# A two-layer RWKV-7 / short-conv / Fourier / MoE block: input projection and units in one written order on all queues, another scratch image for the 32x32 block inverses

## Chip, cores and metric

The kernel runs on one core of a Trainium2 chip. The metric is device time in microseconds (us) from the first to the last instruction of one execution; lower is better.

## The reference, cut to what matters

Two layers. In each, tokens (256 of context, 1024 of latents, 1024 channels) are normalised and multiplied by one wide matrix, the input projection (2944 columns). The first 1920 columns feed a bidirectional RWKV-7 time mixing with 8 heads of 64 channels:

```python
z = z + (shift(z) - z) * mu_shift            # neighbour tokens
r, k, v, lw_f, lw_b, la_f, la_b, lg = split(z)
kk = k * k_k / norm(k * k_k)                 # per head
decay = exp(-exp(-softplus(-(w0 + tanh(lw) @ w2)) - 0.5))
a = sigmoid(a0 + la @ a2);  k_dir = k * (1 + (a - 1) * k_a)
# per direction, over tokens t:
s = s * decay_t - (s @ kk_t) (kk_t * a_t)^T + v_t k_t^T;  y_t = s @ r_t
```

The other columns feed a gated convolution and a Fourier mixing. Then come the output projection, a router and a mixture of 32 experts (top 2), all in float32 accuracy.

## The kernel before, in words

`inproj` does the projection. `project(j, ...)` multiplies one block of 128 output channels (j = 0 to 22) with all 1280 tokens, in chunks of 256, 512 and 512 columns; each chunk is 8 x 3 matmuls, since a float32 product is made from high and low parts (`hh`, `hl`, `wh`, `wl`). `shifted` then makes the token shift of a block by DMAs through the tile `zs`.

The time recurrence is done in chunks of 64 tokens (C). What a chunk needs beforehand is computed in 16 **units** per layer: a unit is (p, hf, d), that is two heads, half of the tokens (10 chunks, 640 tokens) and one direction. The stages of a unit:

- `gates`: two small matmul pairs (`ps<-lw,w` and `ps<-la,a`), tanh on ScalarE (ACT), a scan on VectorE (DVE), two exponentials.
- `heads` (every second unit): the normalised kk. `factors`: the operand tiles `ar` and `bk`. Half of `bk` (lines 532, 533), the sum of `kd` and the spread of `inv` are made on GpSimd (POOL).
- `attn`: 20 products `ps<-ar,bk`, masked by DVE into the two tiles `X` (line 566), and 10 transposes of `bk` into `bt`. DMAs take `ar`, `X` and `bt` to DRAM scratch (`rlD`, `abD`, `btD`, `gD`).

Between them `Pace.feed` puts projection matmuls ("52 units of 512 columns a pass"); I call the time from one unit's gates to the next unit's gates a **pass**.

Each chunk also needs the inverse of a 64x64 triangular matrix, taken from `X` through `gD`. `inverse` inverts 32x32 diagonal blocks, three units at a time (at u = 3, 6, 9, 12), by 60 instructions in a row on GpSimd, one block to a partition. It reads and writes them in an image whose rows of 32 numbers are 64 numbers apart (`diag`), and a transposed copy goes to a second image (`xD`). `merge` loads a unit's blocks again, joins them by 40 small matmuls (`pq<-zt`), and writes `abD`. For units 12 and 13 the inverse runs on VectorE into the tile `lw`, for units 14 and 15 on GpSimd into the tile `v`, in `beside`, which runs next to the scan.

`scan` is the recurrence itself, 20 steps in each direction, and is fed by big loads (`st`) from the scratch. Its first matmuls (`pR<-st`, line 1061) wait for the loads and for two memsets of state on GpSimd (line 1106). After it come `outproj`, `experts` and `combine`.

What sets the order: every engine runs its instructions in program order, and SyncE (SP) issues nearly all DMAs, also in order. In `inproj` the order was made by the framework's scheduler from its own estimates; `in_order` (used in `experts`) pins the written order on all engines but SP.

Of the kernel before, what the change touches and what calls it, by code (L numbers as in the profile page):

```python
# [19 lines left out]
P = 128  # L20
# [20 lines left out]
Q_FIRST, Q_UNIT, Q_TAIL, Q_SCAN, Q_LATE, Q_AT = (40, 35), ((52, 35), (49, 24)), ((40, 60, 40), (20, 60, 40)), 10, 40, (1, 8)  # L41
# [7 lines left out]

Q = 32 * C + 32  # L50
U_ = 2 * Q

# [10 lines left out]
class Pace:  # L63
# [8 lines left out]

    HOLD = 1e9
# [17 lines left out]
    def after(self):  # L91
        return self.tc.issue_after(self.last)

    def one(self, ctx):
        cost = self.cost
        try:
            self.cost = self.stream.send(ctx)
        except StopIteration:
            self.cost = None
        for x in self.later:  # L100
            x[0] -= cost
        while self.later and not self.open and (self.cost is None or self.later[0][0] <= 0):
            self.later.pop(0)[1]()
# [20 lines left out]
class K:  # L124
# [30 lines left out]
    def in_order(self):  # L155
# [9 lines left out]
        for i in traced[start:]:  # L165
            if i.engine == mybir.EngineType.SP:
                continue
# [116 lines left out]
    def weights(self, l, j):  # L284

        hp = self.hp
        wr = hp.tile([P, KD, P], F32, name="wr")
        self.nc.sync.dma_start(wr, self.a["w_in"][l, j])
# [59 lines left out]
    def inproj(self, l, last):  # L348
# [13 lines left out]
        nc.vector.tensor_scalar(om, self.vec("mu", 0, 15), -1.0, 1.0, op0=OP.mult, op1=OP.add)  # L362
        oka = sp.tile([P, 4], F32, name="oka")
        nc.vector.tensor_scalar(oka, self.vec("ka", 0, 4), -1.0, 1.0, op0=OP.mult, op1=OP.add)
# [21 lines left out]
        def project(j, use, ctx=True):  # L386

            wh, wl = self.pre.pop(j) if j in self.pre else self.weights(l, j)
            for c0, n in NCK if ctx else NCK[1:]:
# [11 lines left out]
                pace.open = False  # L401
                between()

# [32 lines left out]
        def shifted(j, name, bufs=1, ctx=True):  # L436
# [14 lines left out]
            else:  # L451
                nc.gpsimd.memset(z[:, :LC], 0.0)
            ts = slice(0, T) if ctx else slice(LC, T)
            nc.scalar.activation(z[:, ts], z[:, ts], AF.Copy, scale=om[:, j:j + 1])
            nc.vector.scalar_tensor_tensor(z[:, ts], zs[:, ts], self.vec("mu", j), z[:, ts], op0=OP.mult, op1=OP.add)
            return z
# [20 lines left out]
        def heads(p, hf, k, inv):  # L477

            kk = un.tile([P, HT], F32, name="kk", bufs=2)
            nc.gpsimd.tensor_copy(kk.rearrange("q (t e d) -> q t e d", e=2, d=64),  # L480
                                 inv[:, 5 * hf:5 * hf + 5, :, None].to_broadcast([P, 5, 2, 64]))
            ps = bank()
            for t in range(5):
                nc.tensor.matmul(ps[:, t * P:(t + 1) * P], kk[:, t * P:(t + 1) * P], self.ident, start=True, stop=True)
# [7 lines left out]
        def gates(p, hf, d, lw, la):  # L492
# [6 lines left out]
            for i, (w, src, dst) in enumerate(((w2, lw, sg), (a2, la, aa))):  # L499
# [8 lines left out]
                nc.vector.tensor_scalar(dst, dst, 0.5, 0.5, op0=OP.mult, op1=OP.add)  # L508
            rev = slice(None, None, -1) if d else slice(None)
            nc.vector.tensor_tensor_scan(flat(sg)[:, rev], rst, flat(sg)[:, rev], 0.0, op0=OP.mult, op1=OP.add)  # L510
            E = un.tile([P, HC, C], F32, name="E")
            Ei = un.tile([P, HC, C], F32, name="Ei")
            nc.scalar.activation(E, sg, AF.Exp, scale=-CC)
            nc.scalar.activation(Ei, sg, AF.Exp, scale=CC)
            return aa, E, Ei

        def factors(p, hf, d, r, k, kk, g, kds):
            aa, E, Ei = g
            rev = slice(None, None, -1) if d else slice(None)
            e0 = 0 if d else C - 1  # L520
            nc.vector.tensor_copy(self.wc[d][:, p, hf * HC:(hf + 1) * HC], E[:, :, e0])
            kd = un.tile([P, HC, C], F32, name="kd", bufs=2)
            nc.scalar.activation(kd, aa, AF.Identity, bias=oka[:, p:p + 1], scale=self.vec("ka", p))
            nc.vector.tensor_tensor(kd, kd, cv(k, hf), op=OP.mult)
            kds.append(kd)
            nc.vector.tensor_tensor(aa, aa, Ei, op=OP.mult)


            ar = un.tile([P, 2, HC, C], F32, name="ar")
            bk = un.tile([P, HC, 2, C], F32, name="bk")  # L530
            lo, hi = slice(0, 64), slice(64, 128)
# [10 lines left out]
            nc.vector.tensor_tensor(ar[:, 1], cv(r, hf), E, op=OP.mult)  # L542
            if len(kds) == 2:
                nc.gpsimd.tensor_tensor(kds[0], kds[0], kds[1], op=OP.add)
                nc.gpsimd.tensor_tensor(kds[0], kds[0], cv(r, hf), op=OP.mult)
                nc.sync.dma_start(self.prD[p][:, hf * HT:(hf + 1) * HT], flat(kds[0]))
            return ar, bk

        def attn(p, hf, d, ar, bk):

            GR = ((0, 5), (5, 5))
            half = lambda e: slice(64 * e, 64 * e + 64)
            img = slice(hf * HC, (hf + 1) * HC)

            Xs = [un.tile([P, 2, HC, C], F32, name="X", bufs=2) for _ in range(2)]
            for c0, n in ((0, 4), (4, 3), (7, 3)):
                ps = bank().rearrange("q (e c s t) -> q e c s t", e=2, s=2, t=C)
                for c in range(n):
                    for e in range(2):
                        h = half(e)  # L560
                        mm = nc.tensor.matmul(ps[:, e, c], bk[h, c0 + c].rearrange("q s t -> q (s t)"), ar[h, :, c0 + c, :],
                                              start=True, stop=True)
                pace.point(mm, W_ATTN)
                for e in range(2):
                    mv = msk[:, d, e].rearrange("q (s t) -> q s t", s=2)
                    nc.vector.tensor_tensor(Xs[e][:, :, c0:c0 + n].rearrange("q s c t -> q c s t"), ps[:, e, :n],
                                            mv[:, None].to_broadcast([P, n, 2, C]), op=OP.mult)
            for e in range(2):
# [1392 lines left out]
```

## Time and profile before

| | us |
|---|---|
| median of 3 runs (3510.56 to 3526.83) | 3520.9 |
| the profiled execution | 3516.07 |
| its span | 3514.3 |
| first gates to first scan matmul, layer 0 / layer 1 | 463.0 / 457.0 |
| first to last gates (15 passes), layer 0 / layer 1 | 364.7 / 354.0 |
| last gates to first scan matmul (the tail), layer 0 / layer 1 | 98.3 / 103.0 |

The last three lines are differences of start times of rows below. Busy shares of the span: TensorE (PE) 89%, DVE 65%, ACT 53%, POOL 32%. TensorE's share counts matmuls with modelled ends, so it also reads high where the clock is low.

### The profile page before, as it was taken

The page shows a single profiled execution, that of the slowest core. Times are in us where ns is not written, and L with a number is a line of the kernel's source. Part 1 is how long each engine was busy: PE and PEld are TensorE (multiplying, and loading weights), DVE is VectorE, ACT ScalarE, POOL GpSimd, SP SyncE. Part 2 cuts the span into 40 slices and gives each one's busy share as a digit, 9 for nine tenths or more (in the row PEclk, how much of TensorE's full clock was granted, in tenths as well). Part 3 has the DMA queues.
Part 4 walks back from the last instruction along what each step waited for, and adds up shares of the span by engine and source line. Part 5 has one row for each costly group of instructions (what it writes and reads, how often), then busy time and mean ns, then how long its engine had stood idle before and what let it go on. Part 6 is the DMA issues. An engine that isn't in the chain of part 4 may idle for free. (4 is left out here: it accounts for less than half of the span.)

```text
span 3514.3 us, 59519 instructions
## 1 busy us (share of the span) xinstructions
PE 3131.3 (89%) x22452; PEld 2446.8 (70%) x22452; DVE 2270.9 (65%) x3540; ACT 1850.8 (53%) x2856; POOL 1141.2 (32%) x1084
## 2 busy tenths in 40 slices
PE   6998888798898999999979988877887989999997
PEld 3777667576676777788736766656666867778884
DVE  4265566233477899988852565563244779998885
ACT  4343433335333777788743434324353467778883
POOL 0026675411222222333200266673013222233330
PEclk8998888899998999999989998778899989999998
DMA  6668889879755999999966678989896488899996
GB/s 248 213 159 176 183 181 194 231 218 328 236 195 191 354 348 339 370 386 382 360 244 231 156 177 177 186 187 247 225 303 199 152 308 327 345 368 376 380 387 230
DMA packets 708063, 922.39 MB, mean 262 GB/s; under 512 B 335074, under 2 KB 561259, under 8 KB 657852
## 3 DMA queue, kind: packets, MB, share of 16 engines
q1 hardware_dynamic: 669456, 871.05, 77.6%
q0 software_dynamic: 38304, 47.49, 4.0%
q8 instruction: 179, 2.93, 0.3%
q14 instruction: 112, 0.92, 0.1%
q10 hardware_dynamic: 12, 0.00, 0.0%
HBM read 726.92 MB, written 203.23 MB: 265 GB/s over the span
## 5 line engine op out<-in xcount | busy, mean ns | idle before, releaser
L176 DVE TENSOR_TENSOR hl<-ld,hl 128x1024 fp32r<-128x1024 f32 x733 | 892.2, 1270 | 30.0 <-ACT hl L175 29.7
L175 ACT ACTIVATE hl<-ld 128x1024 fp32r<-128x1024 f32 x796 | 793.0, 1058 | 22.8 <-PE pR L1572 14.9
L1572 PE MATMUL pR<-hl,wk 128*128 128x512 f32 x1560 | 455.3, 400 | 0.0
L1572 PE MATMUL pU<-hl,wk 128*128 128x512 f32 x1560 | 446.7, 395 | 0.0
L1596 PE MATMUL pA<-hl,wk 128*128 128x512 f32 x1560 | 388.6, 404 | 12.9 <-DVE wk L176 8.9
L397 PE MATMUL pb<-hh,wh 128*128 128x512 f32 (+1 forms) x1000 | 393.0, 394 | 6.7 <-ACT r L430 3.9
L397 PE MATMUL pb<-hl,wh 128*128 128x512 f32 (+1 forms) x1000 | 389.3, 390 | 0.0
L397 PE MATMUL pb<-hh,wl 128*128 128x512 f32 (+1 forms) x1000 | 387.5, 388 | 1.3 <-DVE wl L176 1.3
L1596 PEld LDWEIGHTS pA<-hl,wk 128*128 128x128 f32 x1560 | 290.5, 191 | 98.2 <-ACT wk L175 19.2
L1572 PEld LDWEIGHTS pU<-hl,wk 128*128 128x128 f32 x1560 | 294.4, 189 | 68.0
L1572 PEld LDWEIGHTS pR<-hl,wk 128*128 128x128 f32 x1560 | 288.0, 189 | 61.3 <-ACT wk L175 0.6
L176 POOL TENSOR_TENSOR hl<-ld,hl 128x1024 fp32r<-128x1024 f32 x63 | 176.2, 2797 | 376.0 <-ACT hl L175 376.0
L1603 POOL DMA_INDIRECT yb<-wk,sca x65 | 103.2, 1588 | 472.3 <-ACT wk L1602 437.6
L397 PEld LDWEIGHTS pb<-hh,wh 128*128 128x128 f32 x1000 | 200.3, 200 | 74.2 <-issue 14.8
L397 PEld LDWEIGHTS pb<-hl,wh 128*128 128x128 f32 x1000 | 201.3, 201 | 39.0 <-issue 11.1
L397 PEld LDWEIGHTS pb<-hh,wl 128*128 128x128 f32 x1000 | 200.9, 201 | 35.6 <-issue 3.1
L1276 PE MATMUL pA<-hl,wk 128*128 128x512 f32 x864 | 222.3, 407 | 3.4 <-ACT wk L175 3.3
L1100 POOL DMA_DIRECT2D yD<-yt x72 | 58.1, 807 | 411.5 <-ACT yt L1099 381.1
L1276 PEld LDWEIGHTS pA<-hl,wk 128*128 128x128 f32 x864 | 160.4, 192 | 43.8 <-issue 6.4
L1088 DVE TENSOR_TENSOR tm<-pR,ST 128x256 f32<-128x256 f32 x76 | 32.1, 423 | 237.3 <-PE pR L1083 222.9
L175 ACT ACTIVATE wk<-pm 128x256 fp32r<-128x256 f32 (+1 forms) x195 | 89.0, 456 | 178.2 <-PE pm L1586 115.6
L607 POOL TENSOR_TENSOR gt<-gt,tmp 120x30 f32<-120x30 f32 (+14 forms) x240 | 170.1, 709 | 17.7
(422 smaller groups left out, 5368.2 us busy)
## 6 DMA issues: line engine op xcount, KB each, us to landing
ld<-in_exp_gu SPq DMA_DIRECT2D x260, 1024.0 KB
ld<-in_exp_dn SPq DMA_DIRECT2D x130, 1024.0 KB
st<-rlD SPq DMA_DIRECT2D x80, 512.0 KB
wr<-in_w_in SPq DMA_DIRECT2D x46, 512.0 KB
rlD<-ar SPq DMA_DIRECT2D x64, 320.0 KB
rlD<-X SPq DMA_DIRECT2D x64, 320.0 KB
btD<-bt SPq DMA_DIRECT2D x64, 320.0 KB
st<-abD SPq DMA_DIRECT2D x40, 512.0 KB
```

Of the source, the lines that this page charges most:

```text
L175: nc.scalar.activation(hi, src, AF.Copy)
L176: (eng or nc.vector).tensor_tensor(lo, src, hi.bitcast(F32), op=OP.subtract)
L397: mm = nc.tensor.matmul(ps[:, :n], w[:, k, :], h[:, k, c0:c0 + n], start=(k == 0 and i == 0), stop=(k == KD - 1 and i == 2))
L607: eng.tensor_tensor(gt[:, 0:j, j + 1:32], gt[:, 0:j, j + 1:32], tv, op=OP.add)
L1088: nc.vector.tensor_tensor(tm, RS[:, 1], ST[d], op=OP.add)
L1100: nc.gpsimd.dma_start(self.yD[d][:, ch * C:(ch + 1) * C, :], yt.rearrange("q p d -> q (p d)"))
L1276: nc.tensor.matmul(ps, oo[o][:, k, :], w[k][w_][:, fs], start=(k == 0 and q == 0), stop=(k == KD - 1 and q == 2))
L1572: nc.tensor.matmul(o, x.xT[xi][:, kk, :], w[wi][:, k, :], start=(kk == 0 and i == 0), stop=(kk == KD - 1 and i == 2))
L1596: nc.tensor.matmul(x.y[n], x.h[:, hi_, f, :], dw[wi][:, 0, n * 512:(n + 1) * 512], start=(f == 0 and i == 0), stop=(f == 3 and i == 2))
L1603: nc.gpsimd.indirect_dma_start(out=yb, out_offset=bass.IndirectOffsetOnAxis(ap=x.sca, axis=0), in_=o, in_offset=None, bounds_check=2 * T - ...
```

## The change

It keeps the mathematics and does the following:

1. The whole of `inproj` up to the scan stands in `in_order(True)`, which pins the written order on all queues, SP's DMA issues too. Stages became generators, and the loop places them between groups of projection matmuls by hand. Weights are fetched two blocks ahead.
2. A pass is now: gates of u+1 at its end; `factors`, `attn` of u-1, `heads`, `operands` of u; then the DMAs of `X`, the inverse, the merge.
3. The merge's loads stand in the middle of a pass, its matmuls some 16 projection matmuls later. It makes the transposed block itself (20 more small matmuls), so `xD` and its DMAs are gone.
4. The image: a 32x32 block is 4 KB in one piece, so `inverse` loads and stores whole rows of 4 KB; `attn` writes three 32x32 parts per head (`diag` twice, `corner`) in runs of 128 bytes where it wrote one 64x64 part in runs of 256 bytes.
5. All of `bk`, `kd` and `kk` is made on DVE; one affine step of the gates moves to ACT, one is folded into later operations. The inverse of units 12 and 13 moves from DVE to GpSimd.

```diff
-    def in_order(self):
+    def in_order(self, issue=False):
...
-            if i.engine == mybir.EngineType.SP:
+            if i.engine == mybir.EngineType.SP and not issue:
                 continue
...
-                nc.vector.tensor_scalar(dst, dst, 0.5, 0.5, op0=OP.mult, op1=OP.add)
+                if i == 0:
+                    nc.scalar.activation(dst, dst, AF.Copy, bias=0.5, scale=0.5)
+                yield
...
-            nc.gpsimd.tensor_tensor(bk[hi, :, 0, :], kd[hi], Ei[hi], op=OP.mult)
-            nc.gpsimd.tensor_tensor(bk[hi, :, 1, :], kk[hi, :, rev], aa[hi, :, rev], op=OP.mult)
-            nc.vector.tensor_tensor(bk[lo, :, 1, :], kd[lo], Ei[lo], op=OP.mult)
-            nc.vector.tensor_tensor(bk[lo, :, 0, :], kk[lo, :, rev], aa[lo, :, rev], op=OP.mult)
+            nc.vector.scalar_tensor_tensor(bk[:, :, 1], kk[:, :, rev], 0.5, aa[:, :, rev], op0=OP.mult, op1=OP.mult)
+            for e in range(2):
+                h = slice(64 * e, 64 * e + 64)
+                nc.vector.tensor_tensor(bk[h, :, 2 - 2 * e], kd[h], Ei[h], op=OP.mult)
...
+            for e in range(2):
+                h = slice(64 * e, 64 * e + 64)
+                nc.sync.dma_start(self.rlD[d][e][hf * HC:(hf + 1) * HC, h, p, :].rearrange("m q x -> q m x"),
+                                  ar[h].rearrange("q s (n c) t -> q (s n) (c t)", c=2))
...
+                m = 2 * place[p, hf, d] + e
+                for b in range(2):
+                    q = slice(32 * b, 32 * b + 32)
+                    nc.sync.dma_start(self.diag(m, b), X[h, 0][q, :, q])
+                nc.sync.dma_start(self.corner(m), X[h, 0][0:32, :, 32:64])
...
-                m = (2 * place[p, hf, d] + e) * HC
-                nc.sync.dma_start(self.mats(self.gD, m, HC), X[h, 0])
...
+            img = self.blocks(j0, n)
+            nc.sync.dma_start(gt, img)
...
-                nc.sync.dma_start(self.diag(self.xD, j0, n), xt)
+                nc.sync.dma_start(img, gt.rearrange("q i a -> q (i a)"))
...
-                    inverting = inverse(12, 2, nc.vector, by_l)
...
+        with self.in_order(True):
...
+                a_ = attn(*units[u - 1], *ops) if u else iter(())
+                f_ = factors(p, hf, d, k, g)
+                next(f_)
+                go(a_, 5)
+                next(f_)
+                go(a_, 5)
+                merging = merge(u - 7, lambda: un.tile([P, 1024], F32, name="zt")) if 7 <= u < 16 else None
+                go(a_, 5)
+                f = self.whole(f_)
+                if u % 2 == 0:
+                    kk, kds = heads(p, hf, k, invs[p]), []
+                    pace.free(2 * n)
+                go(a_, 5, 4)
+                ops = operands(p, hf, d, r, kk, f, kds)
+                self.whole(a_)
+                if u % 3 == 0 and u:
+                    if inverting:
+                        inverting()
+                    inverting = inverse(u - 3, 3, nc.gpsimd) if u < 15 else inverse(12, 2, nc.gpsimd, by_l)
+                if merging:
+                    m = merging(nullcontext())
+                    go(m, 6, 6)
+                    self.whole(m)
...
+                    g_ = gates(*units[u + 1], *lw)
+                    go(g_, 7, 7)
+                    g = self.whole(g_)
```

**SP, a pass in the middle of layer 0.** Names are destination and source of a DMA; `nD` is the image of corners. Before:

```order
L573 DMA rlD_61<-X 64x10x128
L575 DMA abD_64<-X 64x5x128
L578 DMA gD<-X 64x10x64
L573 DMA rlD_62<-X 64x10x128
L575 DMA abD_64<-X 64x5x128
L578 DMA gD<-X 64x10x64
L589 DMA btD_66<-bt 128x5x128 x2
L573 DMA rlD_59<-ar 64x10x128
```

Now:

```order
L617 DMA btD_65<-bt 128x5x128 x2
L574 DMA rlD_61<-ar 64x10x128
L574 DMA rlD_62<-ar 64x10x128
L580 DMA prD<-kd 128x640
L625 DMA gD<-X 32x10x32 x2
L626 DMA nD<-X 32x10x32
L627 DMA rlD_59<-X 64x10x128
L629 DMA abD_63<-X 64x5x128
L625 DMA gD<-X 32x10x32 x2
L626 DMA nD<-X 32x10x32
L627 DMA rlD_60<-X 64x10x128
L629 DMA abD_63<-X 64x5x128
```

The DMAs that read the two X tiles stood first and are six; they are ten now and stand behind those of `bt`, of `ar` and of `kd`.

**DVE, the same place, now** (`bk` and `ar` are the operands that the next unit's products read, X the masked products of the last one):

```order
L602 TENSOR_TENSOR X<-ps_5021,msk 128x4x2x64 x2
L602 TENSOR_TENSOR X<-ps_5040,msk 128x3x2x64 x2
L664 MEMSET zt 32x10x32 x2
L602 TENSOR_TENSOR X<-ps_5062,msk 128x3x2x64 x2
L548 SCALAR_TENSOR_TENSOR aa<-aa,Ei 128x640
L549 TENSOR_TENSOR kd<-kd,k 128x640
L559 SCALAR_TENSOR_TENSOR bk<-kk,aa 128x10x64
L562 TENSOR_TENSOR bk<-kd,Ei 64x10x64 x2
L565 TENSOR_TENSOR ar<-kk,E 128x10x63
L566 COPY ar<-kk 128x10
L570 TENSOR_TENSOR ar<-r,E 128x640
```

All six masks now stand ahead of all operand work, in every pass.

**POOL, the end of layer 0's units.** `v` is the inverse of units 14 and 15, `lw` that of 12 and 13 (60 instructions each, cut here), `st` the state memsets of the scan. Before:

```order
L601 MEMSET v 80x32
L605 TENSOR_TENSOR v<-v 80x30
L607 TENSOR_TENSOR v<-v 80x30
...
L605 TENSOR_TENSOR v<-v 80x238
L1106 MEMSET st_5247 64x256 x2
L1106 MEMSET st_5258 64x256 x2
```

Now:

```order
L647 TENSOR_TENSOR v<-v 80x30
L647 TENSOR_TENSOR lw<-lw 80x210
L649 TENSOR_TENSOR v<-v 80x30
L649 TENSOR_TENSOR lw<-lw 80x10x21
...
L649 TENSOR_TENSOR lw<-lw 80x30
...
L649 TENSOR_TENSOR v<-v 80x14x17
L1193 MEMSET st_5801 64x256 x2
L1193 MEMSET st_5812 64x256 x2
```

Before, 27 rows of `v` stand ahead of the memsets; now all 60 of `lw` and 34 of `v` do (in layer 1: 15 before, 60 and 30 now).

## Rows read from the trace of the kernel before

**Rows 1.** Stage: us; busy PE, PEld, DVE, ACT, POOL; PE clock; DMA; GB/s

```profile
335.00:540.00 205.00, 168.25 (x1475) 133.88 (x1474) 115.61 (x149) 78.65 (x117) 142.61 (x171) 0.86 0.88 187
```

**Rows 2.** Timeline of PE: gates of units 0, 1, 15 in both layers

```profile
175.02 1.34 PE L502 MATMUL ps<-lw,w 64*128 64x320 f32 x4
186.17 1.07 PE L502 MATMUL ps<-lw,w 64*128 64x320 f32 x3
539.69 1.34 PE L502 MATMUL ps<-lw,w 64*128 64x320 f32 x4
1961.14 1.07 PE L502 MATMUL ps<-lw,w 64*128 64x320 f32 x3
1974.57 1.34 PE L502 MATMUL ps<-lw,w 64*128 64x320 f32 x4
2315.17 1.07 PE L502 MATMUL ps<-lw,w 64*128 64x320 f32 x3
```

**Rows 3.** PE's waits, 175 to 540, then 1961 to 2315: us, times, longest

```profile
PE pq L645 <- DMA zt<-xD: 22.6, 9, 12.8
...
PE ps L561 <- POOL bk L533: 16.9, 4, 7.4
```

**Rows 4.** Timeline of SP, layers 0 and 1: start, length of issue

```profile
439.08 0.62 SPq L636 DMA_DIRECT2D zt<-xD  x1
...
1989.31 0.63 SPq L573 DMA_DIRECT2D rlD<-X  x1
1989.99 0.64 SPq L575 DMA_DIRECT2D abD<-X  x1
...
2001.79 1.79 SPq L573 DMA_DIRECT2D rlD<-ar  x2
...
2309.43 5.18 SPq L622 DMA_DIRECT2D xD<-zt  x1
...
2329.66 0.59 SPq L578 DMA_DIRECT2D gD<-X  x1
```

**Rows 5.** Timeline of DVE: a mask that waited for an X tile

```profile
2333.17 1.16 DVE L566 TENSOR_TENSOR X<-ps,msk 128x512 f32<-128x512 f32 x2 [3.33 <-DMA gD<-X]
```

**Rows 6.** DVE by form, 175 to 640: count, busy us, mean ns

```profile
L566 DVE TENSOR_TENSOR X<-ps,msk 128x384 f32<-128x384 f32 x64 | 32.5, 549 | 24.2 <-PE ps L561 24.2
L535 DVE TENSOR_TENSOR bk<-kk,aa 64x640 f32<-64x640 f32 x16 | 22.9, 1429 | 0.2
L566 DVE TENSOR_TENSOR X<-ps,msk 128x512 f32<-128x512 f32 x32 | 20.6, 682 | 12.4 <-PE ps L561 12.4
L534 DVE TENSOR_TENSOR bk<-kd,Ei 64x640 f32<-64x640 f32 x16 | 17.3, 1081 | 20.4 <-PE ps L583 20.3
L526 DVE TENSOR_TENSOR aa<-aa,Ei 128x640 f32<-128x640 f32 x16 | 15.6, 975 | 0.0
L537 DVE TENSOR_TENSOR ar<-kk,E 128x630 f32<-128x630 f32 x8 | 10.4, 1300 | 0.0
```

**Rows 7.** Timeline of DVE: masks and an operand step between two inverses on POOL

```profile
328.19 1.02 DVE L566 TENSOR_TENSOR X<-ps,msk 128x384 f32<-128x384 f32 x2
...
334.56 0.82 DVE L535 TENSOR_TENSOR bk<-kk,aa 64x640 f32<-64x640 f32 x1
```

**Rows 8.** Tails: first rows of the inverses, first scan matmuls

```profile
579.56 0.20 DVE L605 TENSOR_TENSOR lw<-lw 80x30 f32<-80x30 f32 x1 [3.96 <-DMA lw<-gD]
...
638.00 0.45 PE L1061 MATMUL pR<-st,st 128*64 128x64 f32 x2 [11.46 <-DMA st<-vE]
...
2418.16 0.44 PE L1061 MATMUL pR<-st,st 128*64 128x64 f32 x2 [12.17 <-DMA st<-vE]
```

**Rows 9.** POOL: `v` alone in its stretch (layer 1), then mean ns by line

```profile
2405.00:2443.00 38.00, 0.00 (x0) 0.00 (x0) 0.00 (x0) 0.00 (x0) 31.09 (x61) 0.68 1.02 282
...
L607 POOL TENSOR_TENSOR gt<-gt,tmp 120x30 f32<-120x30 f32 (+14 forms) x120 | 86.0, 716 | 8.9
...
L607 POOL TENSOR_TENSOR v<-v 80x30 f32<-80x30 f32 (+14 forms) x30 | 15.5, 515 | 2.4
```

More of the change, by code (lines that the diff above doesn't have):

```diff
@@ L71, in __init__ @@
         self.open = False
+        self.pinned = True
     HOLD = 1e9
@@ L101, in one @@
             x[0] -= cost
-        while self.later and not self.open and (self.cost is None or self.later[0][0] <= 0):
+        while self.later and (self.pinned or not self.open) and (self.cost is None or self.later[0][0] <= 0):
             self.later.pop(0)[1]()
@@ L567, in attn @@
                                             mv[:, None].to_broadcast([P, n, 2, C]), op=OP.mult)
+                yield
+            for c0, n in GR:
+                ps = bank().rearrange("q (e c d) -> q e c d", e=2, d=C)
+                for c in range(n):
+                    for e in range(2):
+                        h = half(e)
+                        mm = nc.tensor.matmul(ps[:, e, c], left(e, c0 + c), self.ident[h, h], start=True, stop=True)
+                pace.point(mm, W_ATTN)
+                bt = un.tile([P, 5, P], F32, name="bt", bufs=2)
+                nc.scalar.activation(bt[:, :n].rearrange("q c (e d) -> q c e d", e=2),
+                                     ps[:, :, :n].rearrange("q e c d -> q c e d"), AF.Copy)
+                ch = slice(hf * HC + c0, hf * HC + c0 + n)
+                nc.sync.dma_start(self.btD[d][ch, :, p, :].rearrange("c q x -> q c x"), bt[:, :n])
+                yield
             for e in range(2):
@@ L633, in merge, with steps @@
             for e, (r, o) in enumerate(ro):
-                m = (2 * u + e) * HC
-                nc.sync.dma_start(AM[64 * e:64 * e + 64], self.mats(self.gD, m, HC))
-                nc.sync.dma_start(XP[r], self.mats(self.xD, m, HC)[lo, :, lo])
-            def work(ctx):
+                m = 2 * u + e
+                nc.vector.memset(AM[o, :, lo], 0.0)
+                nc.sync.dma_start(AM[r, :, hi], self.corner(m))
+                for b, (rows, cols) in enumerate(((r, lo), (o, hi))):
+                    nc.sync.dma_start(AM[rows, :, cols], self.diag(m, b))
+            def steps(ctx):
+                pq = qp.tile([P, 512], F32, name=bank)[:, :HC * 32].rearrange("q (u t) -> q u t", t=32)
+                for c in range(HC):
+                    for r, o in ro:
+                        with ctx:
+                            nc.tensor.matmul(pq[r, c, :], AM[r, c, lo], self.ident[r, r], start=True, stop=True)
+                        ctx = nullcontext()
+                for r, o in ro:
+                    nc.scalar.activation(XP[r], pq[r], AF.Copy)
+                yield
                 for st in range(2):
@@ L679, in conv @@
+            yield from shifted(8 + p, "v", then)
         def conv(i):
@@ L832, in inproj @@
                 if u < 15:
-                    inverting = inverse(u - 3, 3, nc.gpsimd)
-                else:
-                    inverting = inverse(12, 2, nc.vector, by_l)
-            if 6 <= u < 15:
-                merging = merge(u - 6, zt)
-            pace.feed(Q_UNIT[last][u > 9])
-        attn(*prev)
-        mg = [merge(9 + i, new, ("pq", "pl")[i % 2]) for i, new in enumerate((x2, x2, lambda: un.tile([P, 1024], F32, name="bk")))]
-        pace.feed(Q_TAIL[last][0])
-        pace.free(Q_TAIL[last][1])
@@ L843, in inproj @@
-        for m in mg:
-            m(pace.after())
-        pace.free(Q_TAIL[last][2])
+                    g_ = gates(*units[u + 1], *lw)
+                    go(g_, 7, 7)
+                    g = self.whole(g_)
+                else:
+                    pace.free(14 * n)
+            a_ = attn(*units[15], *ops)
+            go(a_, 5, 5, 5, 5, 5)
+            self.whole(a_)
+            pace.free(15)
+            mg = [merge(9 + i, new, ("pq", "pl")[i % 2]) for i, new in
+                  enumerate((x2, x2, lambda: un.tile([P, 1024], F32, name="bk")))]
@@ L846, in inproj @@
+            pace.free(15)
+            for m in mg:
+                m = m(nullcontext())
+                go(m, 6, 6)
+                self.whole(m)
+            pace.free(30)
+        pace.pinned = False
         pace.points = []
@@ L861, in beside @@
                 for m in ms:
-                    m(pace.after())
+                    self.whole(m(pace.after()))
             qp.release()
```

229 lines of the change are left out of this document (115 added, 114 removed).

## The prediction, as it stood before the run

> **What bounds the kernel now.** The change touches only the stretch from a layer's first projection matmul to the start of its scan, so I read that stretch: first where its units stand, then what TensorE waits for, then the queue that issues the DMAs.
>
> The starts of the gates [rows 2] cut the stretch. From unit 0 to unit 15 pass 364.7 us in layer 0 (539.69 - 175.02) and 354.0 in layer 1 (2315.17 - 1961.14). The first pass is short, 11.2 and 13.4 us; the other fourteen take 25.3 and 24.3 us on average. From unit 15's gates to the scan's first matmul [rows 8] are 98.3 and 103.0 us, in which PE ends up idle: 11.5 and 12.2 us right ahead of the scan.
>
> In the later passes of layer 0 [rows 1] PE is busy for 168 of 205 us, eight passes, so 21.0 us of a pass, at a granted clock of 0.86 of full (a mix of the levels of 2.4 and 1.2 GHz). No engine is full: DVE 56%, POOL 70%, ACT 38%, DMA 0.88. So it is waits that set the pass. PE's waits [rows 3]: 22.6 us in nine waits for a merge's loads in layer 0, and 16.9 us in four waits for GpSimd's half of `bk` in layer 1. Both are what the new order takes away: the loads get their own lead, and no operand is made on GpSimd.
>
> SP is the queue to look at next. An issue takes about 0.6 us even where little is moved [rows 4], and the transposed image cost one of 5.18 us. What a DMA reads is free for DVE only when it has landed: the issue of `gD<-X` at 2329.66 ended at 2330.25, and the mask that waited for it began at 2333.17 [rows 4, 5], 2.9 us later.
>
> **The change part by part.** 1. *Passes.* Gone are the two waits above, 6 us of a pass at the most. What is late next? In the new SP order the ten DMAs that read the two X tiles stand behind those of `ar`, and the masks of the next pass write the same two tiles. That closes a ring: `ar` done, two DMAs of `ar`, ten of `X`, landing, six masks, operand steps, `ar` done again. Before, the X DMAs stood ahead of `ar`, and the ring was open. I price the ring:
>
> - SP: `ar` twice 1.8, `X` ten times: six small parts at 0.62, two `rlD` at 0.64, two `abD` at 0.8 (an estimate above the 0.64 of the row, for a queue that is busy), and 0.06 between issues: 7.2. The landing 2.9, a semaphore 0.2. Sum 12.1 us.
> - DVE: the first of six masks needs only the first X tile, so five lie on the ring: one of 0.68 and four of 0.55, 2.9 us by [rows 6]; 2.7 by the quiet rows (1.02 for two) [rows 7]. Then `aa` 0.98, `kd` and half of a `kk` taken like it 1.4, `bk` 1.43 and two of 1.08, `ar` 1.30 and, taken like `aa`, 0.98, a small copy 0.4, and 0.5 for the transposes that must have read the old `bk`: 12.0 by the means of [rows 6]. With the 0.82 us that a 640-wide step takes between two inverses [rows 7] it is 9.7. GpSimd now only inverts, and loses the 16 x 2 operand steps, so I take 10.8, nearer to the quiet rows. A weight split or a shift step falls into the ring in about every second pass: 0.6.
>
> 12.1 + 10.8 + 0.6 = 23.5 us. Bounds: 21.2 with all quiet rows and 0.6 less on SP, 27 with the busy ones and two of the longer issues. PE's own work of a pass is below that (21.0 us at clock 0.86, less at a higher one), so the ring decides; PE waits some 2 us of a pass for it, and the clock stays near what it was.
>
> A layer: first pass 13.5 (like 13.4), second 20 (no X tile to wait for: the ring without SP's and the landing's 12.1, plus PE's own 8 or so), then thirteen of 23.5: 339.0 us. Layer 0: 339.0 - 364.7 = -25.7. Layer 1: 339.0 - 354.0 = -15.0.
>
> 2. *Merges.* Twenty more small matmuls a merge; 40 of them took under 1.3 us, so at most 0.7 us, on PE, which waits anyway. If PE were the bound they would cost 0.7 x 9 a layer, 6 us.
>
> 3. *DVE.* One more half of `bk` (1.08) and the `kd` sums in, two affine steps out: they are in the ring above, or (the sums) behind its last step; but the DMA of `kd` stands ahead of X's in every second pass and may add up to 1 us there: in the bounds.
>
> 4. *Image.* The write of 5.18 us [rows 4] and two copies an inverse go. That was SP's time in front of X's DMAs in one of three passes; in the new ring nothing but one issue stands there, so it is already counted. The writes of X are in runs of 128 bytes, not 256. In this trace an issue in runs of 128 bytes took 0.62 us and one in runs of 256 took 0.59 [rows 4], so I charge nothing for the shorter runs, only for the number of DMAs. The Trainium skill, page "DMA: Bandwidth & Descriptors", section "Specifications", speaks against this edit: it puts the smallest transfer at line rate at 512 bytes. By it the six small DMAs would be the slow part of the ring; it is the mechanism of the slower rival below.
>
> 5. *Tail.* `lw` is now on GpSimd, in a row with `v`. Its load stands behind X's DMAs of pass 15, which ends up where it was: 39.9 us after unit 15's gates before [rows 2, 8], and 39 by the ring now. Sixty steps alone took 38 us [rows 9]. Layer 1: `lw` done at 77, then 30 steps of `v`, 19 us, then the memsets: 97. SP meanwhile issues the write of `lw`, nine merge loads and the first scan loads (14 x 0.66 + 2.9 = 12 us, so 89) and is not last. 97 - 103.0 = -6. Layer 0: 40 steps 25 us (64), then twenty of `lw` between twenty of `v`, 25 us (89); SP's 12 us behind that end at 101, the memsets, 14 steps of `v` on, at 98. 101 - 98.3 = +3. The DVE time that `lw` gives back hides nothing: PE is idle there. The GpSimd time is the price of this edit. The same step on GpSimd took 716 ns where DVE was busy, and 515 where it was not [rows 9]; with DVE less busy in the tail I take the second. If it is the first, `lw` costs 9 us more in layer 1 and 13 in layer 0. The Trainium skill, page "SBUF — State Buffer", section "SBUF: two separate sides", says that a GpSimd step and a DVE step with two SBUF inputs lock each other out for a whole instruction; the two rows agree, and its sum would be the dearer one.
>
> Nothing after the scan's start is changed: about the same number of projection matmuls is left over for the scan.
>
> Sum: -25.7 - 15.0 - 6 + 3 = -44 us. Against the profiled execution's 3516.1 us: 3472. The median of the runs is 4.8 us higher, so it would be 3477 from there; I say 3474. A difference of under 0.5% (18 us) is about what a measurement of this kernel can't tell from none.
>
> **The rivals.** *A, the ring is hidden.* If X's DMAs are issued and land faster than I charge (the 21.2 us bound), PE's work sets the pass: 21.0 us at clock 0.86 [rows 1], and a PE that waits less is granted more, so 20.6. That is 2.9 us less in 26 passes, -75: 3399. For it: DMAs of X took 6.2 us where I charge 7.2 plus `ar`. Against it: the mask that did wait for X [rows 5], in an order that gave these DMAs more room.
>
> *B, slower: the queue is the bound.* 21 issues belong to a pass with a merge, six or more to a token shift, one or two to weights: some 28 at 0.65 are 18 us, and a burst of 12 moves 1.8 MB. If the issues stretch as in the 1.79 us of two [rows 4] or the small runs are slow, the ring takes 27 us: 3.5 more in 26 passes, +91: 3565. It decides from 25.2 us a pass on (44 / 26 = 1.7 above my 23.5): there the gain is gone.
>
> *C, no change: the tail eats it.* The dearer GpSimd price (+22), `v` waiting for its load behind eighteen merge loads on SP (12 us, layer 0), and passes at 24 (+13): 3474 + 22 + 13 = 3509, with the load 3521. For it: in both layers the scan's start hangs on POOL rows behind two inverses in one line.
>
> **How the numbers follow.** Forecast, passes of 22.5 to 24.6: 0.45. A 0.19, B 0.17, C 0.19. A and the forecast are faster by over 0.5% but for the upper edge of the forecast's own range (3445 to 3505), C lies within 0.5%, B is slower but for its lower edge: faster 0.63, same 0.20, slower 0.17. To leave out 2 in 10 the range reaches to A's time and to the middle between B's point of decision and its price: 3395 to 3550. Where a case of each sign has weight, the forecast's own range is the 3445 to 3505 above.
>
> **What would show it.** Right: gates 23 to 24 us apart in both layers; DVE's masks waiting for DMAs of X, some 2 us a pass; PE's waits for merge loads and for GpSimd's `bk` gone; the scan's first matmul 97 us after unit 15's gates in layer 1, about 101 in layer 0, with POOL's `v` and SP's loads as what ended last. A shows as gates 20 to 21 us apart with no wait on X, B as gates 26 us apart or more with SP never idle, C as tails of 110 us or more. Wrong I would be above all in the ring: it rests on the length of twelve issues in a row, which this trace shows only six at a time.

## The result and the profile after

The changed kernel takes 3735 us (median of 4 runs, 3720.5 to 3751.5) where the kernel before takes 3522: a ratio of 1.062, 95% interval 1.059 to 1.065. It is 214 us slower. The forecast was 44 us faster, and the range ended at 3550.

The same starts on TensorE as in [rows 2, 8] say where the time went (timeline of PE, changed kernel: gates of units 0 and 15 and the scan's first matmul, both layers):

```profile
172.40 1.34 PE L524 MATMUL ps<-lw,w 64*128 64x320 f32 x4
...
633.62 1.97 PE L524 MATMUL ps<-lw,w 64*128 64x320 f32 x3
...
739.44 0.30 PE L1148 MATMUL pR<-st,st 128*64 128x64 f32 x2 [2.70 <-DMA st<-vE]
...
2068.84 1.34 PE L524 MATMUL ps<-lw,w 64*128 64x320 f32 x4
...
2523.85 1.34 PE L524 MATMUL ps<-lw,w 64*128 64x320 f32 x4
...
2628.94 1.37 PE L1148 MATMUL pR<-st,st 128*64 128x64 f32 x15 [5.99 <-POOL st L1193]
```

The fifteen passes of layer 0 take 461.2 us (633.62 - 172.40), of layer 1 455.0: 96.5 and 101.0 more than before. The tails take 105.8 and 105.1, 7.5 and 2.1 more. These are 207 of the 217 us by which the profiled span (3731.1) is longer. So the passes are what went wrong. After the first two of a layer (16.4 and 22.0 us in layer 0) the other thirteen take 32.5 us each, where I had 23.5.

The stages, in the columns of [rows 1], first those of the kernel before from unit 0's gates to unit 15's, then the same of the changed kernel:

```profile
175.00:540.00 365.00, 321.08 (x2371) 257.52 (x2371) 219.47 (x279) 149.58 (x210) 223.62 (x254) 0.88 0.81 176
1961.00:2315.00 354.00, 306.23 (x2122) 235.61 (x2121) 223.72 (x282) 140.31 (x196) 213.54 (x234) 0.87 0.78 171
...
172.00:634.00 462.00, 402.91 (x3310) 305.40 (x3309) 219.09 (x302) 167.72 (x246) 161.03 (x244) 0.83 0.59 138
2069.00:2524.00 455.00, 396.03 (x3168) 288.77 (x3169) 219.34 (x306) 162.19 (x237) 152.21 (x232) 0.81 0.59 136
```

DMA is at 0.59 in both layers where it had 0.81 and 0.78, POOL at 35% and 33% where it had 61% and 60%, DVE at 47% and 48% where it had 60% and 63%; PE is busy for 87%, about as before, but its ends are modelled and its clock is lower, 0.83 and 0.81 for 0.88 and 0.87. DVE's busy time did not grow (219 us in each layer, for 219 and 224), so what the stage gained is not work of DVE but waiting. The shares do not say for what; DVE's waits do (DVE's waits from layer 0's first gates to layer 1's scan: us, times, longest):

```profile
DVE X L602 <- DMA abD<-X: 161.9, 41, 8.7
...
DVE bk L559 <- PE ps L611: 55.2, 19, 7.4
```

The masks wait 161.9 us for the DMAs that read the X tiles, 5 us a pass; I had 2. One pass of layer 1 shows the whole ring. SP first (timeline of SP: start, length of the issues, count):

```profile
2272.17 1.33 SPq L574 DMA_DIRECT2D rlD<-ar  x2
2273.54 2.96 SPq L625 DMA_DIRECT2D gD<-X  x2
...
2277.69 0.64 SPq L629 DMA_DIRECT2D abD<-X  x1
2278.38 2.04 SPq L625 DMA_DIRECT2D gD<-X  x2
...
2281.61 0.64 SPq L629 DMA_DIRECT2D abD<-X  x1
...
2298.44 0.35 SPq L289 DMA_DIRECT2D wr<-in_w_in  x1
2303.83 1.33 SPq L574 DMA_DIRECT2D rlD<-ar  x2
```

Then DVE, the same stretch:

```profile
2281.53 0.69 DVE L602 TENSOR_TENSOR X<-ps,msk 128x512 f32<-128x512 f32 x1 [7.08 <-DMA abD<-X]
2286.31 1.62 DVE L602 TENSOR_TENSOR X<-ps,msk 128x512 f32<-128x512 f32 x3 [4.09 <-DMA abD<-X]
...
2288.84 1.02 DVE L602 TENSOR_TENSOR X<-ps,msk 128x384 f32<-128x384 f32 x2
...
2290.51 0.82 DVE L549 TENSOR_TENSOR kd<-kd,k 128x640 f32<-128x640 f32 x1
2297.08 1.34 DVE L175 TENSOR_TENSOR wl<-wr,wh 128x1024 fp32r<-128x1024 f32 x1 [5.76 <-ACT wh L174]
2298.34 1.10 DVE L559 SCALAR_TENSOR_TENSOR bk<-kk,aa 128x640 f32<-128x640 f32 x1
...
2303.72 0.54 DVE L571 COPY wc<-E 128x10 f32<-128x10 f32 x1
```

And PE:

```profile
2287.15 1.65 PE L597 MATMUL ps<-ar,bk 64*128 64x128 f32 x12 [7.60 <-DVE X L602]
2290.92 1.33 PE L611 MATMUL ps<-ident,bk 64*128 64x64 f32 x20
2293.45 1.33 PE L611 MATMUL ps<-ident,bk 64*128 64x64 f32 x20
```

Read it as a circle. `ar` is issued at 2272.17 and X's ten DMAs right behind it; the last issue ends at 2282.25. The second X tile is free at 2286.31, 4.06 us later. Only then does DVE write the masks, and PE, which waited 7.60 us for them, goes on in its fixed order: the last products, projection matmuls, twenty half transposes of `bk`, projection matmuls, twenty more, done at 2294.78. The next unit may write `bk` only behind them. Here it waits on until 2298.34, as a weight split stands ahead of it and in turn waits for ACT, whose own split (2296.00) stands behind its copy of those transposes (2294.83). At 2303.83 `ar` is issued again: 31.66 us.

PE's clock around that wait (stages of the same stretch, columns as above):

```profile
2268.00:2279.00 11.00, 11.00 (x63) 7.38 (x62) 5.69 (x9) 6.38 (x8) 0.00 (x0) 1.00 0.44 84
2279.00:2287.00 8.00, 0.55 (x3) 0.12 (x1) 1.38 (x3) 0.60 (x1) 0.00 (x0) 0.81 0.85 185
2287.00:2292.00 5.00, 4.85 (x41) 4.46 (x41) 4.07 (x9) 0.00 (x0) 0.00 (x0) 0.62 0.75 164
2292.00:2298.00 6.00, 4.43 (x56) 3.80 (x55) 0.92 (x1) 2.74 (x4) 4.64 (x13) 0.97 0.49 109
2298.00:2304.00 6.00, 6.00 (x83) 4.64 (x79) 5.97 (x8) 1.77 (x5) 5.61 (x6) 0.50 0.62 186
```

Full clock (2.4 GHz) while PE worked without a gap; then it stood still for most of 8 us and the grant was 0.81, then 0.62 when it went on; and, behind a stretch with gaps at 0.97, 0.50 (1.2 GHz) for 6 us in which it had no gap at all. So a part of what the waits cost comes later, as slower matmuls.

### The profile page after: what moved, and what is told of

The parts are those of the page before. It is cut to its first block, busy times and chain, and to the rows that moved or that the text cites. A ratio compares the mean times of both kernels' runs of the same rounds, so it can differ in the third digit from the quotient of the medians.

```text
span 3731.1 us, 64354 instructions
## 1 busy us (share of the span) xinstructions
PE 3332.2 (89%) x24852; PEld 2570.4 (69%) x24852; DVE 2218.1 (59%) x3491; ACT 1878.0 (50%) x2930; POOL 1005.3 (27%) x1087
## 5 line engine op out<-in xcount | busy, mean ns | idle before, releaser
L406 PE MATMUL pb<-hh,wh 128*128 128x512 f32 (+1 forms) x1000 | 419.2, 419 | 17.6 <-ACT k L449 11.6
L406 PE MATMUL pb<-hh,wl 128*128 128x512 f32 (+1 forms) x1000 | 416.9, 417 | 0.8 <-DVE wl L175 0.8
L406 PE MATMUL pb<-hl,wh 128*128 128x512 f32 (+1 forms) x1000 | 416.5, 417 | 0.0
L406 PEld LDWEIGHTS pb<-hh,wh 128*128 128x128 f32 x1000 | 213.1, 213 | 92.9 <-issue 19.6
L406 PEld LDWEIGHTS pb<-hl,wh 128*128 128x128 f32 x1000 | 213.5, 214 | 46.9 <-issue 13.6
L406 PEld LDWEIGHTS pb<-hh,wl 128*128 128x128 f32 x1000 | 212.5, 212 | 47.6 <-issue 13.4
L602 DVE TENSOR_TENSOR X<-ps,msk 128x384 f32<-128x384 f32 (+1 forms) x192 | 106.4, 596 | 212.0 <-DMA abD<-X 161.9
L597 PE MATMUL ps<-ar,bk 64*128 64x128 f32 x1280 | 114.8, 323 | 98.8 <-DVE X L602 93.9
L614 ACT ACTIVATE bt<-ps 128x640 f32<-128x640 f32 x64 | 45.1, 705 | 281.6 <-PE ps L611 238.0
```

What stands on the lines that cost most here:

```text
L406: mm = nc.tensor.matmul(ps[:, :n], w[:, k, :], h[:, k, c0:c0 + n], start=(k == 0 and i == 0), stop=(k == KD - 1 and i == 2))
L597: mm = nc.tensor.matmul(ps[:, e, c], left(e, c0 + c), ar[h, :, c0 + c, :], start=True, stop=True)
L614: nc.scalar.activation(bt[:, :n].rearrange("q c (e d) -> q c e d", e=2), ps[:, :, :n].rearrange("q e c d -> q c e d"), AF.Copy)
```

## The experiments

The theory is **R**: the pass is set by the ring that X's ten DMAs close, because SP's fixed order has them behind `ar`'s. Rivals: **F/W**, the fixed order of TensorE, DVE and ACT sets the pass whatever SP does; **S**, the DMAs in short runs are slow; **P**, TensorE's own work sets it. Times above the kernel before are differences of medians measured together with it.

| run | edit | us | above the kernel before | ratio, 95% interval |
|---|---|---|---|---|
| | the change | 3735 | 214 | 1.062, 1.059 to 1.065 |
| e1 | X's DMAs right behind the masks | 3590 | 74 | 1.020, 1.016 to 1.025 |
| e2 | X's DMAs ahead of `ar` only | 3624, one run | 108 | |
| e3 | the image's writes twice | 3814, one run | 298 | |
| e4 | SP not in the fixed order | 3626 | 110 | 1.031, 1.029 to 1.034 |
| e5 | e1 and fewer projection matmuls | 3617 | 100 | 1.027, 1.022 to 1.031 |
| e6 | e1 and whole transposes of `bk` | 3571 | 53 | 1.017, 1.011 to 1.022 |
| e7 | e5, e6 and an earlier load | 3564 | 46 | 1.014, 1.012 to 1.016 |
| e8 | the change and fewer matmuls | 3738, one run | 220 | |
| e9 | e7, late inverse on DVE in pieces | 3564 | 47 | 1.016, 1.012 to 1.019 |
| e10 | the kernel before, late inverse on GpSimd | 3537 | 20 | 1.006, 1.004 to 1.008 |
| e11 | e7 with no fixed order | 3546 | 28 | 1.008, 1.006 to 1.010 |
| e12 | e11, late inverse on DVE | 3530 | 15 | 1.004, 1.003 to 1.006 |
| e13 | e12 without e5's edit | 3536 | 14 | 1.005, 1.003 to 1.006 |
| e14 | the change with no fixed order | 3669 | 147 | 1.043, 1.040 to 1.046 |

### e1 and e2: the place of X's DMAs

In e1 the block that issues them moves up in `attn`; in e2 two lines change places:

```diff
 # e1
                 yield
+            for e in range(2):
+                ...
+                    nc.sync.dma_start(self.diag(m, b), X[h, 0][q, :, q])
+                ...
             for c0, n in GR:
 ...
 # e2
-                ops = operands(p, hf, d, r, kk, f, kds)
                 self.whole(a_)
+                ops = operands(p, hf, d, r, kk, f, kds)
```

> Only the place of X's ten DMAs in SP's order moves: right behind the masks, ahead of bt's and ar's. Theory R (the ring by the place in the queue): SP's 10.8 us and the landing's 4.1 leave the pass of 31.6 us; what stays is masks 5.6, to the last transpose of bk 5.3, bk to ar 4.8, 1 us of waits and some 4 to 5 us of TensorE and gates before the next masks, 21 to 23 us. 29 passes by 9.6 us are 278 us: 3455, between 3420 and 3500, and the waits of the masks on DMAs of X (161.9 us) fall below 30. Rival F (the fixed order of TensorE, DVE and ACT makes the pass, whatever SP does): over 3650. Rival S (the short runs make the DMAs slow): the masks go on waiting some 4 us a pass, 3600 to 3700.

> X's ten DMAs stand ahead of ar's two, but still behind bt's, so they wait for the transposes of bk. Theory R: a ring stays, without bk to ar (4.8), ar's issue (2.2) and 1 us of waits, but with ACT's copy to bt and its issue (2 us): about 25.5 us a pass, 6 less in 29 passes, 3560 (3500 to 3620). Rival F: over 3680. Rival S: over 3650.

e1 is 3590, e2 3624, just above its range. Nothing on TensorE, DVE or ACT moved, so F is out as the cause of most of it: 140 of the 214 us hang on where ten DMAs stand in one queue. The masks no longer wait for DMAs; in e2 they still wait 36.6 us for `abD<-X`. The largest of their waits in e1 is now for their own products (DVE's waits, 170 to 2480):

```profile
DVE X L602 <- PE ps L597: 88.9, 50, 6.2
```

But R promised 278 us, and half of it did not come. The stages of e1's passes:

```profile
172.00:577.00 405.00, 377.02 (x3311) 284.15 (x3310) 220.46 (x302) 168.32 (x247) 164.41 (x244) 0.90 0.67 159
1987.00:2384.00 397.00, 365.95 (x3171) 265.67 (x3170) 224.32 (x307) 162.85 (x237) 159.87 (x234) 0.89 0.68 158
```

With the ring open PE is busy for 93% and 92% of the stretch, at 0.90 and 0.89. By these shares TensorE is late next; they are no test of it, and of the runs only e6 below bears on it.

### e3: the image's writes twice

```diff
+                for b in range(2):
+                    q = slice(32 * b, 32 * b + 32)
+                    nc.sync.dma_start(self.diag(m, b, self.gE), X[h, 0][q, :, q])
+                nc.sync.dma_start(self.corner(m, self.nE), X[h, 0][0:32, :, 32:64])
```

> The changed kernel with the six small writes of the image issued twice, the second time to another scratch image that nobody reads. Theory R: six more issues of 0.6 us on the ring in each pass, 29 by 3.6 to 4.2: 105 to 120 us, 3845 (3810 to 3870). Rival F: SP's time is hidden, under 3760. Rival S (bytes in short runs decide, not the issues): the landing grows with the issues, over 3900.

3814 (one run): 84 us more than the change. From the third gates on its passes take 36.2 us in layer 0 ((681.6 - 210.4) / 13, starts of gates) and 34.7 in layer 1 ((2605.7 - 2154.2) / 13), 3.7 and 2.7 more than the change's 32.5 and 32.0. That is 0.45 to 0.6 us for each added issue: the bare issue lies on the ring. S would have had the doubled bytes in short runs cost more than the issues, and the landing grow. Taken pass by pass, as in the table under "Why the prediction was wrong", X's issues take 11.8 us in e3 where they took 8.6, and the landing takes 4.0, no more than the 4.1 there. So the 128-byte runs are not what is slow. The rule of the Trainium skill that the prediction cited against this edit (page "DMA: Bandwidth & Descriptors", section "Specifications") has no price here: SP's issues come first.

### e4 and e14: what the fixed order itself costs

```diff
-        with self.in_order(True):
+        with self.in_order():      # e4: all but SP
+        with nullcontext():        # e14: nothing
```

> The changed kernel with SP left out of the fixed order, so that the scheduler places the DMAs (in its order X's stand ahead of bt's second and of ar's). Theory R: as with X right behind the masks, 3455, between 3420 and 3530, a little more where a load of a weight or a merge comes later. Rival F: over 3650.

> The changed kernel with nothing in a fixed order and no other edit. The scheduler places X's DMAs among ar's and bt's again. If the fixed order is behind what the ring and the other waits cost: 146 less for the ring, 18 for the order of the other engines (eleventh experiment), 3570 (3555 to 3600). If the new parts themselves (image, bk, late inverse) make the loss: over 3650.

e4, 3626, goes R's way but stops short of its range, as e1 did; the masks' wait for `abD<-X` falls from 161.9 to 12.4 us. e14, 3669, is on the other side: without any fixed order the change still loses 147 of its 214 us, so the pinning alone is not the cause, and freeing SP alone gave back more than freeing all. In e14 the masks still wait 45.6 us for X's DMAs (34.9 + 7.2 + 3.5, by the view of their line), and a second tile has taken the place of X (DVE's waits, 170 to 2560):

```profile
DVE zt L664 <- DMA abD<-zt: 81.6, 8, 21.6
```

The memset that a merge now makes on DVE stands ahead of other work and waits up to 21.6 us for the DMA of an earlier merge to have read `zt`. With X's DMAs early in the program (and whole transposes, e5's shares and e7's load), the free order is worth having: e11 below is 3546, the masks wait 7.0 us for DMAs there (5.9 + 1.1), and this memset 37.5. So "fixed or free" alone does not decide. That it is which instruction stands behind a DMA's landing is argued from these waits: the four edits between e14 and e11 were not tried one by one in a free order.

### e5, e6, e8: is it TensorE's work?

```diff
 # e5, e8
-... Q_UNIT ... = ... ((52, 35), (46, 24)) ...
+... Q_UNIT ... = ... ((49, 33), (42, 22)) ...
-            pace.free(15)
+            pace.free((35, 42)[last])
 # e6
-            bk = un.tile([P, HC, 3, C], F32, name="bk")
+            bk = un.tile([P, HC, 2, C], F32, name="bk")
 ...
-                        mm = nc.tensor.matmul(ps[:, e, c], left(e, c0 + c), self.ident[h, h], start=True, stop=True)
+                    mm = nc.tensor.transpose(ps[:, c * P:(c + 1) * P], bk[:, c0 + c].rearrange("q s t -> q (s t)"),
```

> With X's DMAs right behind the masks, as in the first experiment (3590), and the passes with fewer projection matmuls: 672 and 595 of them between the gates of unit 0 and of unit 15, as the kernel before has (675 and 583), in place of 712 and 649; the others go behind the attention of unit 15, where TensorE waits for the inverses. Theory P (with the ring open, TensorE's work sets the pass): 13 and 18 groups of three at 0.75 to 0.9 us leave the passes, 10 and 16 us; the tail of layer 1, where PE is busy 65 of 95 us, takes them for nothing, that of layer 0 (74 of 81) gives back up to 8: 3570, between 3550 and 3585. Rival W (waits of DVE and ACT in their fixed order set the pass): 3590 by 10 to either side.

> X's DMAs right behind the masks, and bk as before the change: two slots a head, so that TensorE transposes it in 10 whole 128x128 steps a unit (0.71 to 0.77 us for five) and not in 40 half ones (1.33 us for twenty); DVE writes it in four half steps and not in one whole and two half ones. Theory P: 1.2 us a pass less on TensorE, 0.8 to 1.1 us more on DVE, which is not full: 30 passes by 0.6 to 1.2 are 18 to 36: 3565, between 3550 and 3580. Rival W: DVE's extra step counts, TensorE's does not: 3600 to 3625.

> The changed kernel with its own place of X's DMAs and only the lighter passes of the fifth experiment. Theory R (the ring sets its pass): of the matmuls taken away those between the masks and the last transpose of bk lie on the ring, a third or so, the others fill TensorE's waits: 5 to 12 us, 3725 (3710 to 3740). Rival P' (TensorE's work sets that pass too): 25 to 30 us, 3700 to 3710.

e5 is no test of what I meant. Its trace has 701 and 631 projection matmuls (counted in 512 columns) between the gates of unit 0 and unit 15's, where e1 has 712 and 649: the shares round up to whole groups, so 11 and 18 moved in place of 40 and 54. The tails, which got all of the 40 and 54, became 13 and 11 us longer, so P and W stay untold by it; e13 shows below that the edit is worth nothing. e8 shows the same for the changed kernel: 3738.

e6 is a test: 19 us less than e1 by the medians (the two intervals overlap), inside P's bounds and far from W's 3600. The edit does two things, whole blocks for halves and `transpose` for `matmul`; the last section tells them apart. Its first term is plain in the rows (timeline of PE, e6; the change's twenty took 1.33, above):

```profile
2262.98 0.74 PE L622 MATMUL ps<-ident,bk 128*128 128x128 f32 x5 [1.66 <-DVE X L602]
...
2289.43 0.71 PE L622 MATMUL ps<-ident,bk 128*128 128x128 f32 x5
```

### e7, e9 to e13: the rest, piece by piece

e7 stacks e5, e6 and an earlier place for the load of the late inverse (`lw`, of units 12 and 14 in the order in which they run; they are places 12 and 13 of the image); e9, e10, e11 and e12 change one thing each:

```diff
 # e7
-                go(a_, 5, 4)
+                go(a_, 5)
+                if u == 15:
+                    inverting()
+                    inverting = inverse(12, 2, nc.gpsimd, by_l)
+                go(a_, 4)
 # e10, in the kernel before
-                    inverting = inverse(12, 2, nc.vector, by_l)
+                    inverting = inverse(12, 2, nc.gpsimd, by_l)
 # e11
-        with self.in_order(True):
+        with nullcontext():
 # e12, on e11
-                    inverting = inverse(12, 2, nc.gpsimd, by_l)
+                    inverting = inverse(12, 2, nc.vector, by_l)
```

> The two edits above together, and the inverse of the late units 12 and 14 loaded right behind X's DMAs of unit 14 and not behind ar's of unit 15 (8 us earlier in a layer, by the trace of the first experiment). Theory P: 20 + 25 + 12 less than 3590: 3533, between 3510 and 3560; about what the kernel before takes (3516), not clearly less. Rival W: over 3580.

> The kernel of the seventh experiment (3564), with the late inverse of units 12 and 14 on DVE again, two or three of its thirty rows at a time between the masks, the weight splits and the merges of the tail; GpSimd then inverts the last two units alone. Theory T (two late inverses in one line on GpSimd hold up the scan): the last inverse ends some 15 to 20 us earlier, and with it the tail and the scan, which the seventh gave 15 us more than the kernel before in each layer: 20 to 40 us, 3530 (3515 to 3545). Rival (the scan's start hangs on TensorE and the merges, the scan itself on its loads): 3555 to 3575.

> The kernel before, with one part of the change alone: the late inverse of units 12 and 14 on GpSimd. Theory T: GpSimd does sixty steps of it in 38 to 45 us and only then, or between them, the last inverse, which ends 15 to 25 us later than now; in both layers the scan waits for it: 3517 + 30 to 45, 3550 (3540 to 3565). Rival (there is slack behind the last inverse): 3517 to 3530.

> The kernel of the seventh experiment (3564) with no queue in a fixed order: the scheduler places the instructions of all engines. Rival W (waits behind instructions that stand at the wrong place in the fixed order are what keeps its passes 17 us a layer longer than those of the kernel before): 3520 to 3545. Theory P (it is the work of TensorE): 3550 to 3590, as the scheduler has the same work to place.

> The kernel of the eleventh experiment (3546; nothing in a fixed order) with the late inverse of units 12 and 14 on DVE, placed by the scheduler. If that inverse on GpSimd costs here what it cost the kernel before alone (20 us): 3526 (3518 to 3536), within 0.5% of the kernel before. If it was worth nothing, as in the ninth experiment: 3540 to 3552. Faster than the kernel before by over 0.5% (under 3500) by neither.

> The kernel of the twelfth experiment (3530, ratio 1.004) with the projection shares of the change again, so without the edit of the fifth, which had moved 11 and 18 matmuls only and had put 40 and 54 more into the tails. If that edit costs here what its median cost the first experiment (27 us), 3505: faster than the kernel before by 0.3%. If the fifth's loss was chance of one build: 3530 by 10.

e7 gave 7 us beyond e6 where 3533 would have been 38, and the profile shows why the terms don't add: its passes are 10 and 23 us shorter than e6's (390.2 and 394.5 to 380.8 and 371.8), but the stretch from unit 15's gates to the end of the scan, which other work bounds too, became 11 us longer in layer 0.

e10 is the one part tried alone in the kernel before: 20 us, less than the 30 to 45 expected, but clear. In layer 1 the scan's first matmul now comes 115 us after unit 15's gates (2435.24 - 2319.82) where it came after 103.0 (timelines of PE and SP, e10):

```profile
2319.82 1.64 PE L502 MATMUL ps<-lw,w 64*128 64x320 f32 x4
...
2419.45 0.32 SPq L618 DMA_DIRECT2D gD<-lw  x1
...
2429.56 1.23 SPq L1047 DMA_DIRECT2D st<-vE  x2
...
2435.24 0.45 PE L1061 MATMUL pR<-st,st 128*64 128x64 f32 x2 [14.67 <-POOL v L605]
```

The row names a step of the inverse `v`, but the state memsets, which the scan waits for on GpSimd, had ended at 2426.14. What landed last is the first load of `vE`, at 2435.15. On SP the scan's loads stand behind the writes of the late inverse. The first of these goes out at 2419.45, as soon as the inverse has ended (2419.42); in the kernel before it went out at 2397.82 (timeline of SP):

```profile
2397.82 0.50 SPq L618 DMA_DIRECT2D gD<-lw  x1
...
2412.81 1.23 SPq L1047 DMA_DIRECT2D st<-vE  x2
```

So the late inverse holds up layer 1's scan by way of SP's queue, and not in the way that theory T had: the last inverse, `v`, was to end 15 to 25 us later, and ends 4 us later (656.7 for 652.9 and 2447.0 for 2443.0). In layer 0 the scan starts no later but takes 20 us longer (291.5 for 271.3, first to last matmul); of that 4 us are left at layer 1's first gates (1965.08 for 1961.14). Put back to DVE it gave nothing in e9, where it stands in pieces by hand: the last inverse ended 11 and 9 us earlier, but the scan began 9 us later. In e12, placed by the scheduler, it gave 13 us (28 to 15 above the kernel before). e11 gave 18 us by freeing all engines, which W had as 19 to 44 and P as none: some of both. e13, without e5's edit, is no different from e12. No version beats the kernel before; e12 comes within 0.4%.

## Why the prediction was wrong

**The bounds of the stage: right, and the ring was seen.** That the passes decide, that X's DMAs behind `ar` close a ring, and that DVE's masks would wait for them, all stand in the trace; e1 undid just that and took 140 of the 214 us with it.

**The step that failed: the price of the ring.** I had 12.1 for SP and the landing, 10.8 for DVE and 0.6 for what falls in between, 23.5. From the starts of the rows shown above, taken for 27 passes, the means are:

| part of the ring | us |
|---|---|
| second tile's first mask to the end of the last mask | 5.7 |
| to the end of the last transpose of `bk` | 5.3 |
| to the first step of the new `bk` | 0.9 |
| to the issue of `ar` | 4.8 |
| issue of `ar` (and of `kd`) | 2.2 |
| ten issues of X | 8.6 |
| landing, to the second tile's first mask | 4.1 |
| sum | 31.6 |

SP and the landing are 14.9, 2.8 above the term: X's ten issues took 8.6 for 7.2, those of `ar` 2.2 for 1.8, the landing 4.1 for 2.9 and the 0.2 of a semaphore, which no row shows by itself. The other half is 16.7 where I had 11.4, and it is not DVE that is slow: from `bk` to `ar` takes 4.8, less than I had by the means of [rows 6]. What I left out is PE inside the ring. The masks, which wait for PE's products, take 5.7 where I had 2.9, and from their end to the new `bk` 6.2 us pass. There I had 2.4 for steps of DVE that run meanwhile, and 0.5 "for the transposes that must have read the old `bk`". In the written order these stand behind groups of projection matmuls, after masks that stand behind such groups too, and PE comes to them late and at a lower clock because it had to wait for the masks. A ring through a queue holds everything that stands ahead in that queue, not only the instructions that need each other. By the sum with 31.6 in thirteen passes the layers would have been forecast at 444 us, against 461 and 455 measured.

**The second step: TensorE's own work.** I had "PE's own work of a pass is below that", and counted twenty more small matmuls a merge and nothing for the transposes. The change makes a unit's ten transposes of `bk` as twenty half ones by `matmul`, each of which is two rows of the trace. They add 1.2 us a pass (twice 1.33 for twice 0.71), 18 a layer. The merges' term was short too: the 40 rows by which I priced it are twenty matmuls, and twenty more took 1.0 us a merge (9.3 us for nine in layer 0) where I had 0.7 at most. And the passes hold 37 and 66 more projection matmuls than before (712 and 649 for 675 and 583). So rival A's price, PE at 20.6 us, was not there to be had: in e1, with the ring open and PE busy for 93% and 92%, the passes take 27 to 28 us from the third on. How much of that is PE's work and how much waits in the fixed order stays open: e6 gave 21 us with intervals that overlap, e11 gave 18.

**Small runs.** Right to charge the issues alone (e3).

**The tail.** The steps were sized right: sixty steps of `lw` took 37 us in layer 1 where I had 38, and the memsets ended up behind `v` as said, behind 32 of its rows where I had 30 (timeline of POOL, changed kernel):

```profile
2570.63 0.15 POOL L643 MEMSET lw<- 80x32 f32 x1 [37.79 <-DMA lw<-gD]
...
2607.83 0.23 POOL L649 TENSOR_TENSOR lw<-lw 80x30 f32<-80x30 f32 x1
...
2628.58 1.38 POOL L1193 MEMSET st<- 64x256 f32 x4
```

The load landed 46.8 us after unit 15's gates, not 39, since the ring stands ahead of it too: +2 for the -6 forecast, and in layer 0 +7.5 for +3. What I did not see is that the same edit costs the kernel before 20 us (e10). I had SP as "not last" ahead of layer 1's scan; there it is SP's loads, behind the late inverse's write, that start the scan 12 us later.

**The rivals.** B had the slower side with 27 us a pass and SP as the bound. The pass is longer, but SP is not the bound: it stood idle for 5.0 us ahead of `ar` at 2303.83. C's 110 us tails did not come.

**What stays open.** The runs give back 214 - 15 us in steps: 140 for the place of X's DMAs, 21 for the transposes (with intervals that overlap), 7 for e7, 18 for the free order, 13 for the late inverse (steps under 10 us are within the noise of the medians). The last 15 were not taken apart; e12's passes are still 7 and 22 us longer than before, and its scans 16 and 20. Its passes also hold more projection matmuls (737 and 733 for 675 and 583), so their lengths do not compare like for like. Whether another pair of X tiles would open the ring was not tried.

## What to carry to other kernels

When a queue is pinned to a written order, put the DMAs that read a reused tile where the tile becomes ready, ahead of anything that needs a later result; and price the circle from the reuse to itself with everything that stands between on every queue it passes. If a change makes a stage longer and most of its engines emptier, look for the longest wait, and follow it to see whether it returns to its own cause. Where the profile names a releaser, check that the instruction which waited needs it: in e10 it named a step that the scan does not read. An open ring is worth only the way to the next bound, so price that too before promising the whole.

## What the runs showed of the hardware

A float32 transpose made as a `matmul` with the identity cost TensorE nearly twice one made as `transpose`, and cutting it into halves cost next to nothing. In the kernel before, five whole blocks took 1.27 us by `matmul` and 0.71 by `transpose` (timeline of PE, kernel before):

```profile
181.63 1.27 PE L484 MATMUL ps<-ident,kk 128*128 128x128 f32 x10
...
204.73 0.71 PE L583 MATMUL ps<-ident,bk 128*128 128x128 f32 x5
```

A `matmul` of the program is two rows in this trace, a `transpose` is one: five calls are x10 in the first line and x5 in the second. The changed kernel's ten half blocks by `matmul`, x20, took 1.33 us, about what five whole ones took that way. Their rows start in pairs 7 ns apart, a pair about every 111 ns (2290.922 and 2290.929, then 2291.082 and 2291.089, 2291.194 and 2291.200). The Trainium skill, page "TensorE: Matmul & The Clock Gate", section "Wait — 56ns, not 53.3ns?", gives a floor of about 62 ns a matmul for one of two ways of decoding; starts 7 ns apart lie under it, so it is not what these rows show.
